# Attention by pairs of heads on the two halves of the array

## The chip, the cores and the metric

One core of a Trainium2 chip runs the whole program in one launch. The metric is the device time of a run in microseconds (us), the median of three runs. The engines have short names in the profile: PE (TensorE, matrix products), PEld (its weight loads), DVE (VectorE), ACT (ScalarE), POOL (GpSimd) and SP (which issues the DMAs). One matrix product needs its stationary operand loaded into the 128 x 128 array and streams the moving operand through it. A product whose operands cover 64 rows, or whose result covers 64 columns, takes half the array.

## The reference

Two blocks of two layers each work on 512 tokens of width 1024. Attention is 8 heads of width 64 in both.

```python
# block 1, per layer: window of 128 with a sink; head h reads key/value group h // 4
s = einsum(q_block, k_band) * 64 ** -0.5          # query block of 128 against 2 x 128 keys
p = softmax(concat([where(mask, s, -inf), sink]))[..., :-1]
ya = (p @ v_band) @ w_a
r = chunkwise_retention(rq, rk, rv)               # 4 heads
x = x + (sigmoid(ga) * ya + sigmoid(gb) * (norm(r) * silu(rg)) @ w_b) @ w_out
x = x + square(relu(norm(x) @ w_up)) @ w_down
# block 2, per layer: an indexer selects keys, then attention, then gated linear attention
score = einsum(relu(q_idx . k_idx), w_idx)        # 8 index heads of width 64
p = softmax(where(in_top_128(score), q k / 8, -inf)); ya = (p @ v) @ p_attn
state = decay * state + k_dec^T v; o = q state    # chunks of 64 tokens, 4 heads
```

## The kernel before, in words

Activations lie feature-major: eight tiles of 128 features by 512 tokens. Products with the big weights run in three passes (`k_step`, lines 387 to 394): operands are split into a high and a low part, and high x high, low x high and high x low are added in PSUM. A main unit is one output tile: 8 input tiles x 3 passes = 24 products of 512 columns (`fm`, line 404); in `tm` (line 435) it is a token tile against 256 weight columns, 24 products of 256 columns, with a burst behind every second one.

All small work is run beside these units by `Pump` (lines 214 to 252), which has six lanes. A job is a generator that alternates between a step that issues products and a step that issues what reads them. After each main unit `unit_done` (line 370) calls `products()`, which takes one products step of every lane in lane order, so that these products stand in TensorE's queue as one burst behind the unit; then it emits the unit's own evacuation, then `results()`, and then `top_up`, the split of the next weight piece into high and low (ACT line 328, DVE line 329). Everything is in program order on its engine; a wait in a burst holds the next main unit too.

An attention job has three products steps: the scores (`mm3`, lines 396 to 402, three passes of 64 rows), the transposes of the probabilities (line 541), and the products with V (lines 612 and 1088, results of 64 columns; each is two instructions, since these operands are plain float32). Between scores and transposes lies the softmax: mask and maximum on DVE (578 and 1069), exponential on ACT (589 and 1075), reciprocal and scaling on DVE (546 and 548).

- `attn1` (line 561, block 1): one job takes one query block of 128 tokens and two heads of the same key group; both heads' scores use the same 64 rows. 16 jobs per layer in lanes 0 to 2. The two heads' products with V go to different halves of the columns (`64 * j`, line 613).
- `attn2` (line 1057, block 2): one job takes one query block b with 128 * (b + 1) keys. For b < 2 it holds two heads (h0 and h0 + 2, which lie in the same half), for b >= 2 one. 24 jobs per layer in lanes 0 to 2.
- `index` (line 1023): per pair of heads three passes of the even head (rows 0 to 63), then three of the odd one (rows 64 to 127), in two PSUM banks.
- `gla` (line 1155): per 128 tokens two chunks c of 64 tokens, each on its half of the rows: 6 products of c = 0, then 6 of c = 1, twice; then 8 products with the states (line 1195), c outermost.

PSUM has 2 banks for main units and 6 for the side work (`side_ps`).

Of the kernel before, what the change touches and what calls it, by code (L numbers as in the profile page):

```python
# [19 lines left out]
P = 128  # L20
# [9 lines left out]
PAD = 24  # L30
# [42 lines left out]
def _weights_1(a, l):  # L73
    w = a["w_in"][l]
    aq = w[:, 0:512].reshape(D, 8, 64)[:, :, _ROPE]
    aq = np.stack([aq[:, 0:4], aq[:, 4:8]], axis=2).reshape(D, 512)
    ak = w[:, 512:640].reshape(D, 2, 64)[:, :, _ROPE].reshape(D, 128)
    s = []
    s += _fm(aq) + _fm(ak) + _fm(w[:, 640:768])
    s += _fm(w[:, 768:1280]) + _fm(w[:, 1280:1792])  # L80
    s += _tm(w[:, 1792:2816])
    s += _fm(w[:, 3840:4864])
    s += _fm(a["w_a"][l])
# [79 lines left out]
def layout(a):  # L163
# [11 lines left out]
    for l in range(DEPTH):  # L175
        sm.add(f"g_mix{l}", _cols(a["g_mix"][l]))
        sm.add(f"g_mlp{l}", _cols(a["g_mlp"][l]))
        sm.add(f"sink{l}", np.broadcast_to(a["sinks"][l][None, :], (P, 8)))
# [76 lines left out]
class Net:  # L255
# [287 lines left out]
    def normalize(self, sp, parts, sm):  # L543

        rc = self.tiny(len(parts))
        self.nc.vector.reciprocal(rc, sm)
        for i, s in enumerate(parts):
            self.nc.vector.tensor_scalar(sp[:, s], sp[:, s], rc[:, i : i + 1], None, op0=ALU.mult)

    def head_done(self, st, f, n):  # L550

        st["pv"][f][1] += n
        if st["pv"][f][1] == 8:
# [7 lines left out]
    def attn1(self, b, f, aq, st, l):  # L561

        nc = self.nc
        g, i = f // 2, f % 2
        nk = 1 if b == 0 else 2
        w = nk * P
        r = slice(64 * g, 64 * g + 64)
        at = [slice(j * 256, j * 256 + w) for j in range(2)]
        ps = self.side_ps()
        for j in range(2):  # L570
            self.mm3(
                ps[:, at[j]], aq[2 * i + j], st["ak"], r,
                slice(b * P, (b + 1) * P), slice((b + 1 - nk) * P, (b + 1) * P),
            )
        yield
        sp, mr, sm = self.s(), self.tiny(2), self.tiny(2)
        for j in range(2):
            nc.vector.tensor_tensor_reduce(
                out=sp[:, at[j]], in0=ps[:, at[j]],
                in1=self.band[:, 256 - w : 256], scale=1.0, scalar=-3.0e38,  # L580
                op0=ALU.add, op1=ALU.max, accum_out=mr[:, j : j + 1],
            )
        sink = self.small(f"sink{l}")[:, 2 * f : 2 * f + 2]
        m, nm, d = self.tiny(2), self.tiny(2), self.tiny(2)
        nc.vector.scalar_tensor_tensor(m, mr, 0.125, sink, op0=ALU.mult, op1=ALU.max)
        nc.vector.tensor_scalar(nm, m, -1.0, None, op0=ALU.mult)
        nc.vector.tensor_tensor(d, sink, m, op=ALU.subtract)
        for j in range(2):
            nc.scalar.activation(
                sp[:, at[j]], sp[:, at[j]], AF.Exp,  # L590
                bias=nm[:, j : j + 1], scale=0.125, accum_out=sm[:, j : j + 1],
            )
        nc.scalar.activation(d, d, AF.Exp)
        nc.vector.tensor_tensor(sm, sm, d, op=ALU.add)
        self.normalize(sp, at, sm)
        yield
        pt = self.side_ps()
        for s in at:
            self.transposes(pt[:, s], [sp[:, s.start + k * P : s.start + (k + 1) * P] for k in range(nk)])
        yield  # L600
        PT = self.s()
        if nk == 2:
            nc.scalar.copy(PT, pt)
        else:
            for s in at:
                nc.scalar.copy(PT[:, s], pt[:, s])
        yield
        pv = self.head_bank(st, f)
        for j in range(2):
            for k in range(nk):  # L610
                o = (b + 1 - nk + k) * P + 64 * g
                nc.tensor.matmul(
                    pv[64 * j : 64 * j + 64, b * P : (b + 1) * P], lhsT=st["V"][:, o : o + 64],
                    rhs=PT[:, at[j].start + k * P : at[j].start + (k + 1) * P], start=(k == 0), stop=(k == nk - 1),
                )
        yield
        self.head_done(st, f, 2)
        yield

# [92 lines left out]
    def layer_1(self, l, x, nx):  # L712
# [30 lines left out]
        def ev_kv(o, ps):  # L743
# [7 lines left out]
            else:  # L751
                av = self.s()
                nc.vector.tensor_tensor(av, ps, st["R"], op=ALU.mult)
                self.pump.add(0, self.vtrans(av, st, "V"))
                n = 0
                for f0 in (0, 2):
                    for b in range(4):
                        for f in (f0, f0 + 1):
                            if 0 < n < 3:
                                self.pump.add(n, self.idle(3-n))  # L760
                            self.pump.add(n % 3, self.attn1(b, f, aq, st, l))
                            n += 1
# [260 lines left out]
    def index(self, b, iq, st):  # L1023
# [33 lines left out]
    def attn2(self, b, hs, aq, ak, st):  # L1057

        nc = self.nc
        n = (b + 1) * P  # L1060
        r = slice(64 * (hs[0] % 2), 64 * (hs[0] % 2) + 64)
        at = [slice(i * n, (i + 1) * n) for i in range(len(hs))]
        ps = self.side_ps()
        for s, h in zip(at, hs):
            self.mm3(ps[:, s], aq[h // 2], ak[h // 2], r, slice(b * P, (b + 1) * P), slice(0, n))
        yield
        sp, mr, sm, nm = self.s(), self.tiny(len(hs)), self.tiny(len(hs)), self.tiny(len(hs))
        for i, s in enumerate(at):
            nc.vector.tensor_tensor_reduce(
                out=sp[:, s], in0=ps[:, s], in1=st["bias"][b], scale=1.0, scalar=-3.0e38,  # L1070
                op0=ALU.add, op1=ALU.max, accum_out=mr[:, i : i + 1],
            )
        nc.vector.tensor_scalar(nm, mr, -0.125, None, op0=ALU.mult)
        for i, s in enumerate(at):
            nc.scalar.activation(sp[:, s], sp[:, s], AF.Exp, bias=nm[:, i : i + 1], scale=0.125, accum_out=sm[:, i : i + 1])
        self.normalize(sp, at, sm)
        yield
        pt = self.side_ps()
        w = n * len(hs)
        self.transposes(pt, [sp[:, k * P : (k + 1) * P] for k in range(w // P)])  # L1080
        yield
        PT = self.s()
        nc.scalar.copy(PT[:, :w], pt[:, :w])
        yield
        for s, h in zip(at, hs):
            pv = self.head_bank(st, h // 2)
            for k in range(b + 1):
                nc.tensor.matmul(  # L1088
                    pv[64 * (h % 2) : 64 * (h % 2) + 64, b * P : (b + 1) * P], lhsT=st["V"][k][:, h * 64 : (h + 1) * 64],
                    rhs=PT[:, s.start + k * P : s.start + (k + 1) * P], start=(k == 0), stop=(k == b),  # L1090
                )
        yield
        for h in hs:
            self.head_done(st, h // 2, 1)
        yield

    def gla_gates(self, glr, wg, gk, st):
# [4 lines left out]
        for t0 in (0, 2):  # L1102
            pp = [self.side_ps(), self.side_ps()]
            for i in range(2):
                t = t0 + i
                self.mm3(pp[i], glr, wg, slice(0, 33), slice(t * P, (t + 1) * P), FULL)
# [48 lines left out]
    def gla(self, gq, kd, gv, st):  # L1155
# [8 lines left out]
        for t in range(4):  # L1164
            kds, gvs = nxt
            pk = [[self.side_ps(), self.side_ps()] for _ in range(2)]
            for i in range(2):
                for c in range(2):
                    r = slice(64 * c, 64 * c + 64)
                    for j in range(2):  # L1170
# [20 lines left out]
            for i in range(2):  # L1191
                for c in range(2):
                    for j in range(2):
# [29 lines left out]
    def layer_2(self, l, xs, iq, wgd, last):  # L1223
# [83 lines left out]
        for h0 in (0, 4):  # L1307
            even, odd = (h0, h0 + 2), (h0 + 1, h0 + 3)
            for b in range(4):
                for hs in (even, odd) if b < 2 else ((h0,), (h0 + 1,), (h0 + 2,), (h0 + 3,)):  # L1310
                    if n < 3:
                        self.pump.add(n, self.wait([3], n))
                    self.pump.add(n % 3, self.attn2(b, hs, aq, ak, st))
                    n += 1
# [269 lines left out]
def emit(nc, meta, arrays, stop=None):  # L1584
# [4 lines left out]
    with tile.TileContext(nc) as tc:  # L1589
        with (  # L1590
# [8 lines left out]
            stack.enter_context(tc.tile_pool(name="pad", bufs=1)).tile([P, PAD], F, name="pad")  # L1599
# [53 lines left out]
```

## Time and profile before

| | us |
|---|---|
| median of 3 runs (3393.69 to 3393.78) | 3393.76 |
| the profiled execution's own time | 3394.25 |
| its span | 3392.5 |
| PE busy | 3348.3 (99%) |
| PEld busy | 2818.3 (83%) |
| DVE busy | 1965.2 (58%) |
| ACT busy | 1292.1 (38%) |
| POOL busy | 657.0 (19%) |

The span is the time between the first and the last instruction of the profiled execution; its own time is 1.75 us longer. The ends of matmuls are modelled and overlap the next, so that PE's busy share tells that it hardly stands still, not that each product is at its fastest. In the timeline the first column is the start of an instruction; what a product costs is the distance to the next start. The granted clock is 0.996 of full speed on the mean.

### The profile page before, as it was taken

What the parts mean: (1) busy time and instruction counts of PE and PEld (TensorE: products, weight loads), DVE (VectorE), ACT (ScalarE), POOL (GpSimd) and SP (SyncE); (2) the same over time, 40 slices, a digit from 0 to 9 for tenths busy, and PEclk for the clock granted to TensorE, in tenths of its full rate; (3) what the DMA queues carried; (4) which work ended last, traced back from release to release, by engine and by line L of the source; (5) the groups of instructions that cost most, each with busy time, mean ns of one, the idle gap of its engine ahead of it and who ended that gap; (6) DMA issues with size and microseconds to landing.
All of it is one profiled execution on the core that took longest, in us unless ns stands there. A gap on an engine that the chain in (4) does not pass through costs nothing.

```text
span 3392.5 us, 43066 instructions
## 1 busy us (share of the span) xinstructions
PE 3348.3 (99%) x17450; PEld 2818.3 (83%) x17450; DVE 1965.2 (58%) x3435; ACT 1292.1 (38%) x2206; POOL 657.0 (19%) x447
## 2 busy tenths in 40 slices
PE   9999999999999999999999999999999999999998
PEld 7888888887888888889988778888889777888887
DVE  7555543457555553456884447555778744575466
ACT  3433333233333343333533344343354333443342
POOL 5100000123100010031550013210146400232113
PEclk9999999999999999999999999999999999999998
DMA  4222222232122222231212131223212122312230
GB/s 150 75 75 78 97 100 100 99 125 75 51 75 75 100 103 97 91 136 52 81 70 75 63 124 50 87 100 126 98 52 75 63 75 75 124 41 97 100 137 26
DMA packets 44935, 295.93 MB, mean 87 GB/s; under 512 B 5120, under 2 KB 7296, under 8 KB 10816
## 3 DMA queue, kind: packets, MB, share of 16 engines
q1 hardware_dynamic: 44496, 292.66, 24.1%
q8 instruction: 137, 2.24, 0.3%
q14 instruction: 62, 0.51, 0.0%
q0 software_dynamic: 80, 0.26, 0.0%
q10 hardware_dynamic: 160, 0.26, 0.0%
HBM read 291.06 MB, written 2.10 MB: 86 GB/s over the span
## 4 chain that ended last, share of the span: by engine, by line
PE 92%; DVE 5%; issue 1%; ACT 1%; POOL 0%; DMA 0%; DVEq 0%; SPq 0%; ACTq 0%; POOLq 0%
PE pm L392 22%; PE pm L393 22%; PE pm L394 22%; PE ps L392 3%; PE ps L394 3%; PE ps L393 3%; PE pm L445 3%; PE pm L446 3%; PE pm L447 3%; PE ps L541 2%; PE ps L400 1%; PE ps L1088 1%; DVE s L1008 1%; PE ps L401 1%; PE ps L402 1%
## 5 line engine op out<-in xcount | busy, mean ns | idle before, releaser
L392 PE MATMUL pm<-xh,hi 128*128 128x512 f32 (+1 forms) x3056 | 1193.4, 391 | 3.8 <-DVE c L1407 3.0
L393 PE MATMUL pm<-xl,hi 128*128 128x512 f32 (+1 forms) x3056 | 1181.4, 387 | 1.6 <-DVE xl L1560 1.1
L394 PE MATMUL pm<-xh,lo 128*128 128x512 f32 (+1 forms) x3056 | 1180.7, 386 | 0.4 <-DVE lo L329 0.4
L392 PEld LDWEIGHTS pm<-xh,hi 128*128 128x128 f32 x3056 | 573.9, 188 | 127.3 <-issue 12.3
L394 PEld LDWEIGHTS pm<-xh,lo 128*128 128x128 f32 x3056 | 573.9, 188 | 118.5 <-DVE lo L329 0.8
L393 PEld LDWEIGHTS pm<-xl,hi 128*128 128x128 f32 x3056 | 574.3, 188 | 115.5 <-DVE xl L1560 3.2
L329 DVE TENSOR_TENSOR lo<-raw,hi 128x1024 fp32r<-128x1024 f32 (+1 forms) x413 | 516.8, 1254 | 173.0 <-ACT hi L328 172.2
L328 ACT CAST hi<-raw 128x1024 fp32r<-128x1024 f32 (+1 forms) x469 | 483.0, 1035 | 205.7 <-PE pm L393 165.3
L445 PE MATMUL pm<-hi,xh 128*128 128x256 f32 x768 | 221.0, 288 | 0.8 <-DVE s L1006 0.7
L446 PE MATMUL pm<-lo,xh 128*128 128x256 f32 x768 | 217.3, 283 | 0.0
L447 PE MATMUL pm<-hi,xl 128*128 128x256 f32 x768 | 217.1, 283 | 0.0
L392 PE MATMUL pm<-xh,whi 128*128 128x512 f32 (+1 forms) x512 | 186.6, 365 | 4.1 <-DVE s L534 4.1
L393 PE MATMUL pm<-xl,whi 128*128 128x512 f32 (+1 forms) x512 | 186.2, 364 | 0.8 <-DVE xl L1560 0.5
L394 PE MATMUL pm<-xh,wlo 128*128 128x512 f32 (+1 forms) x512 | 185.4, 362 | 0.0
L1415 POOL TENSOR_TENSOR c<-c,c 128x512 f32<-128x512 f32 x44 | 84.3, 1916 | 500.7 <-DVE c L1407 477.6
L329 POOL TENSOR_TENSOR lo<-raw,hi 128x1024 fp32r<-128x1024 f32 x56 | 140.8, 2515 | 128.8 <-ACT hi L328 108.7
L445 PEld LDWEIGHTS pm<-hi,xh 128*128 128x128 f32 x768 | 147.1, 192 | 8.0 <-issue 2.7
L446 PEld LDWEIGHTS pm<-lo,xh 128*128 128x128 f32 x768 | 147.3, 192 | 0.2
L447 PEld LDWEIGHTS pm<-hi,xl 128*128 128x128 f32 x768 | 147.2, 192 | 0.0
L392 PE MATMUL ps<-xh,hi 128*128 128x512 f32 (+1 forms) x384 | 138.7, 361 | 7.3 <-ACT hi L328 7.3
L498 POOL TENSOR_TENSOR s<-s,s 128x512 f32<-128x512 f32 x26 | 34.9, 1343 | 567.7 <-ACT s L495 567.5
L1406 DVE SCALAR_TENSOR_TENSOR c<-pm,smalls,c 128x511 f32<-128x511 f32 x82 | 61.4, 749 | 135.0 <-ACT c L1405 134.8
(318 smaller groups left out, 4779.3 us busy)
## 6 DMA issues: line engine op xcount, KB each, us to landing
raw<-w SPq DMA_DIRECT2D x265, 1024.0 KB, 4.8
raw<-w SPq DMA_DIRECT2D x7, 768.0 KB, 4.4
x<-x SPq DMA_DIRECT2D x8, 256.0 KB, 7.0
out<-acc SPq DMA_DIRECT2D x16, 128.0 KB, 1.8
raw<-w SPq DMA_DIRECT2D x2, 896.0 KB, 4.5
s<-big SPq DMA_DIRECT2D x6, 256.0 KB, 5.6
raw<-w SPq DMA_DIRECT2D x2, 512.0 KB, 5.1
smalls<-small SPq DMA_DIRECT2D x1, 462.5 KB, 7.5
```

Of the source, the lines that this page charges most:

```text
L328: self.nc.scalar.copy(hi[:, :n], raw)
L329: e.tensor_tensor(lo[:, :n], raw, hi[:, :n].bitcast(F), op=ALU.subtract)
L392: mm(ps[:, ts], lhsT=w1, rhs=xh[:, ts], start=first, stop=False)
L393: mm(ps[:, ts], lhsT=w1, rhs=xl[:, ts], start=False, stop=False)
L394: mm(ps[:, ts], lhsT=w2, rhs=xh[:, ts], start=False, stop=last)
L445: self.nc.tensor.matmul(ps[:, :256], lhsT=x1, rhs=w1, start=(k == 0), stop=False)
L446: self.nc.tensor.matmul(ps[:, :256], lhsT=x1, rhs=w2, start=False, stop=False)
L447: self.nc.tensor.matmul(ps[:, :256], lhsT=x2, rhs=w1, start=False, stop=(k == NK - 1))
L498: (e or self.nc.gpsimd).tensor_tensor(acc, acc, sq, op=ALU.add)
L541: self.nc.tensor.transpose(dst[:, i * P : (i + 1) * P], src, self.ident)
L1406: nc.vector.scalar_tensor_tensor(c[:, 1:], ps[:, : T - 1], w[1], c[:, 1:], op0=ALU.mult, op1=ALU.add)
L1415: nc.gpsimd.tensor_tensor(a, a, c, op=ALU.mult)
```

## The change

One function `attend` takes the place of `attn1`'s and `attn2`'s bodies. A job now takes one pair f of heads, one on each half of the rows (g = 0 and 1), and one or two query blocks. Scores of the two heads go to two banks, pass by pass in turn; the probabilities are transposed into two banks; the products with V take turns between the two column halves. In block 1 a pair is a head of key group 0 and the same head of key group 1 (the rows of `w_a` are put in that order on the host), and a job takes blocks (0, 1) or (2, 3): 8 jobs per layer in lanes 0 and 1. In block 2 a job takes blocks (0, 1), (2) or (3): 12 jobs per layer in lanes 0 and 1. The width of the unused tile `pad` is computed so that what follows the table of small constants keeps its address.

```diff
-    def mm3(self, ps, a, b, rows, ca, cb):
-        (ah, al), (bh, bl) = a, b
-        mm(ps, lhsT=ah[rows, ca], rhs=bh[rows, cb], start=True, stop=False)
-        mm(ps, lhsT=ah[rows, ca], rhs=bl[rows, cb], start=False, stop=False)
-        mm(ps, lhsT=al[rows, ca], rhs=bh[rows, cb], start=False, stop=True)
+    def mm3(self, *jobs):
+        for i, j in ((0, 0), (0, 1), (1, 0)):
+            for ps, a, b, rows, ca, cb in jobs:
+                mm(ps, lhsT=a[i][rows, ca], rhs=b[j][rows, cb], start=(i == j), stop=(i == 1))
...
-        if st["pv"][f][1] == 8:
+        if st["pv"][f][1] == 4:
...
+    def attend(self, f, blocks, q, k, v, st, sink=None):
+        nc = self.nc
+        segs, o = [], 0
+        for b, k0, nk, mask in blocks:
+            segs.append((b, k0, nk, mask, slice(o, o + nk * P)))
+            o += nk * P
+        rows = [slice(0, 64), slice(64, P)]
+        ps = [self.side_ps(), self.side_ps()]
+        for b, k0, nk, mask, at in segs:
+            self.mm3(*[
+                (ps[g][:, at], q, k, rows[g], slice(b * P, (b + 1) * P), slice(k0 * P, (k0 + nk) * P))
+                for g in range(2)
+            ])
+        yield
+        n = 2 * len(segs)
+        sp, mr, sm, nm = [self.s(), self.s()], self.tiny(n), self.tiny(n), self.tiny(n)
+        parts = [(g, sg[3], sg[4]) for g in range(2) for sg in segs]
+        for i, (g, mask, at) in enumerate(parts):
+            nc.vector.tensor_tensor_reduce(
+                out=sp[g][:, at], in0=ps[g][:, at], in1=mask, scale=1.0, scalar=-3.0e38,
+                op0=ALU.add, op1=ALU.max, accum_out=mr[:, i : i + 1],
             )
...
+        for i, (g, mask, at) in enumerate(parts):
+            nc.scalar.activation(
+                sp[g][:, at], sp[g][:, at], AF.Exp,
+                bias=nm[:, i : i + 1], scale=0.125, accum_out=sm[:, i : i + 1],
             )
+        if sink is not None:
+            nc.scalar.activation(d, d, AF.Exp)
+            nc.vector.tensor_tensor(sm, sm, d, op=ALU.add)
+        rc = self.tiny(n)
+        nc.vector.reciprocal(rc, sm)
+        for i, (g, mask, at) in enumerate(parts):
+            nc.vector.tensor_scalar(sp[g][:, at], sp[g][:, at], rc[:, i : i + 1], None, op0=ALU.mult)
+        yield
+        pt = [self.side_ps(), self.side_ps()]
+        for g in range(2):
+            self.transposes(pt[g], [sp[g][:, j * P : (j + 1) * P] for j in range(o // P)])
+        yield
+        PT = [self.s(), self.s()]
+        for g in range(2):
+            nc.scalar.copy(PT[g][:, :o], pt[g][:, :o])
         yield
         pv = self.head_bank(st, f)
+        for b, k0, nk, mask, at in segs:
+            for j in range(nk):
+                for g in range(2):
+                    nc.tensor.matmul(
+                        pv[rows[g], b * P : (b + 1) * P], lhsT=v(k0 + j, g),
+                        rhs=PT[g][:, at.start + j * P : at.start + (j + 1) * P], start=(j == 0), stop=(j == nk - 1),
+                    )
+        yield
+        self.head_done(st, f, len(segs))
+        yield
...
+                self.pump.add(1, self.idle(2))
                 n = 0
+                for f in range(4):
+                    for bs in ((0, 1), (2, 3)):
+                        self.pump.add(n % 2, self.attn1(f, [band(b) for b in bs], aq, st, l))
+                        n += 1
...
-            for h, ps in zip((h0, h0 + 1), pss):
-                r = slice(64 * (h % 2), 64 * (h % 2) + 64)
-                self.mm3(ps[:, :n], iq[h // 2], st["ik"], r, slice(b * P, (b + 1) * P), slice(0, n))
+            self.mm3(*[
+                (ps[:, :n], iq[h0 // 2], st["ik"], slice(64 * g, 64 * g + 64), slice(b * P, (b + 1) * P), slice(0, n))
+                for g, ps in enumerate(pss)
+            ])
...
             for i in range(2):
-                for c in range(2):
-                    r = slice(64 * c, 64 * c + 64)
-                    for j in range(2):
-                        h = 2 * i + j
-                        js = slice(j * 256, (j + 1) * 256)
-                        self.mm3(pk[i][c][:, js], kds, gvs[i], r, slice(h * P, (h + 1) * P), js)
+                for j in range(2):
+                    h = 2 * i + j
+                    js = slice(j * 256, (j + 1) * 256)
+                    self.mm3(*[
+                        (pk[i][c][:, js], kds, gvs[i], slice(64 * c, 64 * c + 64), slice(h * P, (h + 1) * P), js)
+                        for c in range(2)
+                    ])
...
-                for c in range(2):
-                    for j in range(2):
+                for j in range(2):
+                    for c in range(2):
                         js = slice(j * 256, (j + 1) * 256)
...
+        for f in range(4):
+            for bs in ((0, 1), (2,), (3,)):
+                if n < 2:
+                    self.pump.add(n, self.wait([3], n))
+                self.pump.add(n % 2, self.attn2(f, bs, aq, ak, st))
+                n += 1
```

## Rows read from the trace of the kernel before

**Rows 1.** The page: busy time, share of the span and instructions of each engine.
```profile
PE 3348.3 (99%) x17450; PEld 2818.3 (83%) x17450; DVE 1965.2 (58%) x3435; ACT 1292.1 (38%) x2206; POOL 657.0 (19%) x447
```
**Rows 2.** PE's longest wait: engine, line, releaser; us in total, times, longest.
```profile
PE ps L1195 <- DVE S L1185: 7.6, 2, 3.8
```
**Rows 3.** Timeline of PE, block 2's first scores: start, us, engine, line, form.
```profile
1812.08 0.39 PE L393 MATMUL pm<-xl,hi 128*128 128x512 f32 x1
1812.30 0.39 PE L394 MATMUL pm<-xh,lo 128*128 128x512 f32 x1
...
1813.12 0.27 PE L401 MATMUL ps<-xl,xh 64*128 64x128 f32 x1
1813.23 0.27 PE L402 MATMUL ps<-xh,xl 64*128 64x128 f32 x1
...
1813.77 0.39 PE L393 MATMUL pm<-xl,hi 128*128 128x512 f32 x1
```
**Rows 4.** Timeline of PE, a burst of index scores.
```profile
1615.64 0.39 PE L394 MATMUL pm<-xh,lo 128*128 128x512 f32 x1
...
1616.53 0.40 PE L402 MATMUL ps<-xh,xl 64*128 64x512 f32 x2
1616.76 0.35 PE L400 MATMUL ps<-xh,xh 64*128 64x384 f32 x2
1616.94 0.34 PE L401 MATMUL ps<-xl,xh 64*128 64x384 f32 x2
...
1617.42 0.28 PE L401 MATMUL ps<-xl,xh 64*128 64x256 f32 x2
1617.54 0.28 PE L402 MATMUL ps<-xh,xl 64*128 64x256 f32 x2
...
1618.09 0.40 PE L393 MATMUL pm<-xl,hi 128*128 128x512 f32 x1
```
**Rows 5.** Timeline of PE, block 1's products with V alone in a burst.
```profile
186.42 0.39 PE L394 MATMUL pm<-xh,lo 128*128 128x512 f32 x1
186.74 0.67 PE L612 MATMUL ps<-s,V 128*64 128x128 f32 x8
...
187.68 0.40 PE L393 MATMUL pm<-xl,hi 128*128 128x512 f32 x1
```
**Rows 6.** Timeline of PE, a burst of block 2's attention with all kinds of work.
```profile
1888.53 0.39 PE L394 MATMUL pm<-xh,lo 128*128 128x512 f32 x1
...
1890.18 1.09 PE L1088 MATMUL ps<-s,V 128*64 128x128 f32 x8
1891.92 0.39 PE L393 MATMUL pm<-xl,hi 128*128 128x512 f32 x1
```
**Rows 7.** Timeline of PE, linear attention's 24 products of one burst.
```profile
1737.64 0.39 PE L394 MATMUL pm<-xh,lo 128*128 128x512 f32 x1
...
1739.36 0.28 PE L402 MATMUL ps<-xh,xl 64*128 64x256 f32 x2
...
1740.26 0.39 PE L393 MATMUL pm<-xl,hi 128*128 128x512 f32 x1
```
**Rows 8.** Timeline of DVE, softmax of a block 1 job (two heads).
```profile
82.37 0.41 DVE L578 CUSTOM_DVE_ANT_0 s<-ps,s 128x256 f32<-128x256 f32 x1
...
86.28 0.61 DVE L548 TENSOR_SCALAR s<-s,t 128x256 f32<-128x256 f32 x2
```
**Rows 9.** Timeline of PE, that job's transposes, first of their burst.
```profile
88.78 0.49 PE L541 MATMUL ps<-smalls,s 128*128 128x128 f32 x3
```
**Rows 10.** Timeline of ACT, that job's first exponential.
```profile
84.67 0.51 ACT L589 ACTIVATE s<-s,t 128x256 f32<-128x256 f32 x1 [8.40 <-DVE t L586]
```
**Rows 11.** Timeline of DVE, softmax of a block 2 job (one head, 512 keys).
```profile
1899.88 0.69 DVE L1069 CUSTOM_DVE_ANT_0 s<-ps,score 128x512 f32<-128x512 f32 x1 [0.18 <-PE ps L402]
...
1901.90 0.49 DVE L548 TENSOR_SCALAR s<-s,t 128x512 f32<-128x512 f32 x1
```
**Rows 12.** Timeline of PE, the first product of the burst behind it.
```profile
1905.85 0.32 PE L400 MATMUL ps<-xh,xh 64*128 64x128 f32 x1
```

More of the change, by code (lines that the diff above doesn't have):

```diff
@@ L29 @@
 AHEAD_1, AHEAD_2 = 9, 11
-PAD = 24
 TOP_ROUNDS = 2
@@ L177, in layout @@
         sm.add(f"g_mlp{l}", _cols(a["g_mlp"][l]))
-        sm.add(f"sink{l}", np.broadcast_to(a["sinks"][l][None, :], (P, 8)))
+        pairs = np.repeat(a["sinks"][l].reshape(2, 4).T, 2, axis=1).reshape(1, 16)
+        sm.add(f"sink{l}", np.broadcast_to(pairs, (P, 16)))
     sm.add("g_final", _cols(a["g_final"]))
@@ L559, in head_bank @@
         return st["pv"][f][0]
-    def attn1(self, b, f, aq, st, l):
+    def attend(self, f, blocks, q, k, v, st, sink=None):
         nc = self.nc
[L564 to L569, printed above, removed]
-        for j in range(2):
-            self.mm3(
-                ps[:, at[j]], aq[2 * i + j], st["ak"], r,
-                slice(b * P, (b + 1) * P), slice((b + 1 - nk) * P, (b + 1) * P),
-            )
-        yield
-        sp, mr, sm = self.s(), self.tiny(2), self.tiny(2)
-        for j in range(2):
[L578 to L595, printed above, removed]
-        yield
[L597 to L606, printed above, removed]
@@ new lines, in attend @@
+        sp, mr, sm, nm = [self.s(), self.s()], self.tiny(n), self.tiny(n), self.tiny(n)
[4 more added lines that the diff above has]
+                op0=ALU.add, op1=ALU.max, accum_out=mr[:, i : i + 1],
+            )
+        if sink is None:
+            nc.vector.tensor_scalar(nm, mr, -0.125, None, op0=ALU.mult)
+        else:
+            m, d = self.tiny(n), self.tiny(n)
+            nc.vector.scalar_tensor_tensor(m, mr, 0.125, sink, op0=ALU.mult, op1=ALU.max)
+            nc.vector.tensor_scalar(nm, m, -1.0, None, op0=ALU.mult)
+            nc.vector.tensor_tensor(d, sink, m, op=ALU.subtract)
@@ L607, in attn1 @@
+        yield
+        pt = [self.side_ps(), self.side_ps()]
+        for g in range(2):
+            self.transposes(pt[g], [sp[g][:, j * P : (j + 1) * P] for j in range(o // P)])
+        yield
+        PT = [self.s(), self.s()]
+        for g in range(2):
+            nc.scalar.copy(PT[g][:, :o], pt[g][:, :o])
         yield
         pv = self.head_bank(st, f)
[L609 to L615, printed above, removed]
+        for b, k0, nk, mask, at in segs:
[4 more added lines that the diff above has]
+                        rhs=PT[g][:, at.start + j * P : at.start + (j + 1) * P], start=(j == 0), stop=(j == nk - 1),
+                    )
@@ L616, in attn1 @@
         yield
-        self.head_done(st, f, 2)
+        self.head_done(st, f, len(segs))
         yield
+    def attn1(self, f, blocks, aq, st, l):
+        v = lambda k, g: st["V"][:, k * P + 64 * g : k * P + 64 * g + 64]
+        yield from self.attend(f, blocks, aq[f], st["ak"], v, st, self.small(f"sink{l}")[:, 4 * f : 4 * f + 4])
     def vtrans(self, src, st, key):
@@ L754, in ev_kv @@
                 self.pump.add(0, self.vtrans(av, st, "V"))
+                band = lambda b: (b, max(0, b - 1), min(b + 1, 2), self.band[:, 128 if b == 0 else 0 : 256])
+                self.pump.add(1, self.idle(2))
                 n = 0
[L756 to L762, printed above, removed]
+                for f in range(4):
+                    for bs in ((0, 1), (2, 3)):
+                        self.pump.add(n % 2, self.attn1(f, [band(b) for b in bs], aq, st, l))
+                        n += 1
         self.fm(xs, 2, ev_kv)
@@ L1055, in index, with attn2 @@
             yield
[L1057 to L1095, printed above, removed]
+    def attn2(self, f, bs, aq, ak, st):
+        v = lambda k, g: st["V"][k][:, f * P + 64 * g : f * P + 64 * g + 64]
+        yield from self.attend(f, [(b, 0, b + 1, st["bias"][b]) for b in bs], aq[f], ak[f], v, st)
     def gla_gates(self, glr, wg, gk, st):
@@ L1191, in gla @@
             for i in range(2):
-                for c in range(2):
-                    for j in range(2):
+                for j in range(2):
+                    for c in range(2):
                         js = slice(j * 256, (j + 1) * 256)
@@ L1306, in layer_2 @@
         n = 0
[L1307 to L1314, printed above, removed]
+        for f in range(4):
[4 more added lines that the diff above has]
+                n += 1
         sil, tga, tgb = [None] * 8, [None] * 8, [None] * 8
@@ L1598, in emit @@
             smalls = const.tile([P, arrays["small"].shape[1]], F, name="smalls")
-            stack.enter_context(tc.tile_pool(name="pad", bufs=1)).tile([P, PAD], F, name="pad")
+            pad = (24 - (arrays["small"].shape[1] - 928)) % P or P
+            stack.enter_context(tc.tile_pool(name="pad", bufs=1)).tile([P, pad], F, name="pad")
             hi = stack.enter_context(tc.tile_pool(name="hi", bufs=HI_BUFS))
```

10 lines of the change are left out of this document (2 added, 8 removed).

## The prediction

> **What bounds the kernel now.** I read the page's busy shares first: PE is busy 99% of the span, DVE 58%, ACT 38% [rows 1]. Then the waits of PE: the longest group is 7.6 us, in linear attention, and the change leaves what it waits for as it is [rows 2]. So TensorE's queue sets the time, and a product that takes fewer nanoseconds there shortens the run, as long as what the product reads is ready. What is left is to see what a product costs, and for that the timeline is read by the distance from one start to the next. Main products follow each other at 0.22 to 0.23 us (1812.08 to 1812.30 [rows 3]; I take 0.227, a unit of 24 being 5.45 us). From the last product of a unit to the second one of the next there would be two such steps, 0.454 us, without a burst; what is more is the burst's cost.
>
> Four prices come out. (a) Scores of one head: 128 columns follow at 0.11 us (1813.12 to 1813.23) [rows 3]. (b) Scores in the index: the rows say x2. Products of the two halves start together and the pair takes one step: 0.23 us for 512 columns (1616.53 to 1616.76), 0.18 for 384, 0.12 for 256 [rows 4]. There, program order is three products of one half, then three of the other. The two halves run side by side all the same. (c) Products with V: eight instructions take 0.67 us in block 1, whose two heads write different column halves [rows 5], and 1.09 us in block 2, whose heads write one half or come alone [rows 6]. (d) Each change between full-array and half-array work, or between row halves and column halves, costs extra. A burst of six scores alone costs 1813.77 - 1812.30 - 0.454 = 1.01 us, of which 6 x 0.11 = 0.66 are steps: 0.35 for two changes, 0.175 each [rows 3]. The burst of [rows 6] has 8 transposes (0.11 a step, as three last 0.49 with one of 0.27 [rows 9]), 3 scores of 512 and 8 instructions with V at 0.11: 3.39 - 0.454 less 0.88, 0.69 and 0.88 is 0.49, or 0.16 for each of three changes. Transposes use the full array and change nothing beside a main product. I take 0.175.
>
> **The change part by part.** All counts are from the loops, the two layers of each block taken together.
>
> *Scores of block 1.* Per layer 24 products of 128 columns and 72 of 256, one after another: 24 x 0.11 + 72 x 0.12 = 11.3 us. In pairs half of that goes; two layers save 11.3 us.
>
> *Scores of block 2.* Per head 3 x (0.11 + 0.12 + 0.18 + 0.23) = 1.92 us, eight heads 15.4; half goes in each of two layers: 15.4 us. No row shows a pair of 128 columns. Its step lies between 0.11 (as a 256-column pair keeps the single's step) and 0.22 (no overlap); the second would take back 24 pairs x 0.11 x 2 blocks = 5.3 us. I take 0.11, the nearest row being the 256-column pair.
>
> *Products with V.* Block 1 is paired already, so nothing changes. Block 2 has 16 heads (two layers) x 10 products x 2 instructions = 320, that is 40 times eight; each eight goes from 1.09 to 0.67: 40 x 0.42 = 16.8 us.
>
> *Bursts and changes of the array.* Before, a layer of block 1 has 18 bursts (59.69 to 186.74 us in the first layer) and block 2 has 26 (1812.62 to 2006.99), with three lanes in different steps. Written out by kind and counted, they have 53 and 82 changes. After, two lanes hold 4 and 6 jobs of three steps each, the second lane one unit later: 13 and 19 bursts. They run in cycles of (transposes, scores), (V, transposes), (scores, V), with 2 + 2 + 3 changes, or 29 and 43 in all. That saves 2 x (53 + 82 - 29 - 43) = 126 changes x 0.175 = 22.0 us. The transposes keep their number.
>
> *What pairs cost.* An index burst costs 1618.09 - 1615.64 - 0.454 = 2.00 us with 3 x 0.53 = 1.59 in steps, so 0.41 for its two changes against 0.35 for single scores [rows 3, 4]. I charge the 0.06 to each of the 40 new jobs (8 x 2 and 12 x 2): 2.4 us.
>
> *Index scores.* They are x2 before the edit, so taking turns in program order gains nothing [rows 4]: 0, with 0.1 us either way for each of ten bursts. The Trainium skill speaks otherwise: "TensorE: Matmul & The Clock Gate", section "The mechanism" of Part 3, says matmuls start and end in strict program order and only weight loads are pulled ahead of them. By that rule only one product of three would overlap before the edit; the trace disagrees, as the second half's first product starts with the first half's first one.
>
> *Linear attention.* Six products of one half stand ahead of six of the other, and the rows turn to x2 only after the third. A burst costs 1740.26 - 1737.64 - 0.454 = 2.17 us [rows 7]. With all 24 in pairs it is 12 x 0.12 + 0.41 = 1.85. Eight such bursts save 2.6 us. The products with the states (line 1195) wait for DVE's states, whose order stays [rows 2]: 0, between a loss of 0.4 and a gain of 0.6 us for each of eight bursts.
>
> *Softmax.* A job's softmax now has two heads and up to four parts between two bursts, and TensorE stands if the transposes come first. In block 1 two parts of 256 run from 82.37 to 86.89 [rows 8], ahead of the transposes at 88.78 [rows 9]. Two more add 2 x 0.35 (mask and maximum, 0.41 long with overlap), 2 x 0.5 (exponential [rows 10]) and 2 x 0.31 (scaling [rows 8]) = 2.3: 89.2. The new bursts are shorter, so that the transposes would be called at about 88.6 and the second bank's 0.4 later. Such a job is late by some 0.2 us. This holds for the 5 jobs per layer beside units whose evacuation is rope on DVE, 10 in all: 2 us. Bounds: 0, if DVE has no other delay, and 15, if a weight split (some 1.2 us on DVE) falls into the chain each time. In block 2 the softmax of 512 keys ends at 1902.39, 3.5 us ahead of the next burst [rows 11, 12]; a second head adds 0.6 + 0.7 + 0.5 = 1.8, and the shorter burst takes about 1: still early, 0.
>
> Splits, evacuations and DMAs move with their units and are hidden under PE; the softmax has fewer small operations, which DVE has room for [rows 1].
>
> **Sum.** 11.3 + 15.4 + 16.8 + 22.0 - 2.4 + 2.6 - 2.0 = 63.7 us off the profiled execution's 3394.25: 3330.6. The median lies 0.5 lower, so 3330 us.
>
> **Rivals.**
>
> *Softmax late in block 1.* DVE's evacuation, weight split and the four-part chain fill a whole unit, so each of the 10 jobs holds TensorE by 1.5 us instead of 0.2: 3330 + 13 = 3343. For it: two parts already end only 1.9 us ahead [rows 8, 9]. Against: every third unit has no softmax and catches up. "TensorEngine Tiling (Array Packing)", section "PSUM Bottleneck", of the Trainium skill warns of the same: tiling speeds the products, not what reads their banks.
>
> *The pairs don't run together in the attention jobs,* so the change doesn't do what it says. Then scores, V and linear attention save nothing, only the 22.0 of array changes less 2.0 remain: 3374. For it: no row shows attention scores in pairs. Against: index and block 1's V do it [rows 4, 5].
>
> *Slower.* In both blocks the transposes wait for the softmax of two heads in all 40 jobs. It decides from 65.7 / 40 = 1.6 us a job (the gain without the 2 us charged above); at 2.5 us it takes 100, and the time is 3394 - 66 + 100 = 3428. For it: one chain through DVE, ACT and DVE, twice as wide. Against: block 2 has 3.5 us in hand [rows 11, 12].
>
> *Array changes cheaper still.* If a pair's first step hides its change, the 2.4 and part of the 29 + 43 changes go too (2 x 72 x 0.05 = 7): 3321.
>
> *Products start in program order after all,* and the starts in the rows x2 are not when the halves really work. Then an index burst of six products of one width cost five steps and will cost three; a layer's index has 8 x 3 x (0.12 + 0.18 + 0.23) = 12.7 us of single steps, a third of it goes in each of two layers, 8.5 us: 3322. That is the skill's rule cited at the index. Against: 2.00 us for 18 products, which single steps of 3.2 us don't allow, nor five sixths of them, 2.65 [rows 4].
>
> **Chances.** Forecast 70%, softmax late 15%, pairs apart 4%, slower 4%, cheaper changes 5%, program order 2%. The forecast's own range is 3324 to 3338; the stated one reaches to the cheaper changes and the late softmax, 3320 to 3350, and takes in the unseen pair (5.3) and the states (-3 to +5); with some 15% outside. About 0.2% (7 us) is what a measurement tells from no change; all but the slower case lie clear of it, with 1% left between.
>
> **What would show it.** After, attention scores in the timeline say x2; eight V instructions of block 2 take 0.67 us; bursts number 13 and 19 a layer; index bursts cost 2.0 as before; linear attention's 24 products cost 1.85. A wait of PE on line 541's transposes for DVE's scaling, above 0.2 us a job, shows the late softmax. Single scores in the new jobs, or PE's idle time above 40 us, would make it wrong.

## The result, and the profile after

The changed kernel takes 3336.05 us (median of four runs, 3334.57 to 3336.14), the kernel before 3393.73 beside it. The ratio is 0.983 [0.9813, 0.9847]: a gain of 57.7 us. The prediction said 63.7 us less and 3330; the time is 6 us above that. The profiled execution is the fastest of the four, 3334.57 us, at a mean granted clock of 0.996; against the profiled execution of before, 3394.25, that is 59.7 us.

TensorE is still the engine that sets the time; its busy share is 98% where it was 99% [rows 1]:

```profile
PE 3280.2 (98%) x17450; PEld 2771.7 (83%) x17450; DVE 1931.4 (58%) x3307; ACT 1285.0 (39%) x2182; POOL 657.1 (20%) x447
```

The same 17450 instructions take 68.1 us less of TensorE's time. DVE and ACT have fewer instructions, as the softmax's small operations now serve twice as many parts (a head in one query block) at a time.

Now the four kinds of small products, in the timeline of TensorE after (start, us, engine, line, form). First the index, linear attention, block 2's first scores and its last products with V:

```profile
1599.70 0.39 PE L394 MATMUL pm<-xh,lo 128*128 128x512 f32 x1
1600.02 0.50 PE L402 MATMUL ps<-xh,xh 64*128 64x512 f32 x2
...
1602.14 0.40 PE L393 MATMUL pm<-xl,hi 128*128 128x512 f32 x1
...
1721.69 0.39 PE L394 MATMUL pm<-xh,lo 128*128 128x512 f32 x1
1722.01 0.38 PE L402 MATMUL ps<-xh,xh 64*128 64x256 f32 x2
...
1723.96 0.40 PE L393 MATMUL pm<-xl,hi 128*128 128x512 f32 x1
...
1795.88 0.39 PE L394 MATMUL pm<-xh,lo 128*128 128x512 f32 x1
1796.19 0.33 PE L402 MATMUL ps<-xh,xh 64*128 64x128 f32 x2
1796.36 0.28 PE L402 MATMUL ps<-xl,xh 64*128 64x128 f32 x2
1796.47 0.28 PE L402 MATMUL ps<-xh,xl 64*128 64x128 f32 x2
...
1797.42 0.39 PE L393 MATMUL pm<-xl,hi 128*128 128x512 f32 x1
...
1930.88 1.09 PE L610 MATMUL ps<-s,V 128*64 128x128 f32 x16
```

Read each as in the prediction: the distance from the main product ahead to the second one behind, less 0.454. The index costs 1602.14 - 1599.70 - 0.454 = 1.99, as before [rows 4]. Linear attention's 24 products cost 1.82 where they took 2.17 [rows 7]. Block 2's first job now says x2, and its pairs of 128 columns follow each other at 0.11 us (1796.36 to 1796.47): the pair that no row of before showed costs what a single product costs [rows 3]. With V, sixteen instructions take the 1.09 us that eight took [rows 6].

Added up over all bursts in that way, from the two timelines (where the main products have 256 columns, their step is about 0.11 in place of 0.227, and less is taken off): block 1's two layers go from 65.6 to 47.7 us (13 bursts a layer), block 2's from 110.6 to 65.3 (19 a layer; the transposes for other work that share these bursts are left out on both sides), linear attention's eight from 17.4 to 14.6. That is 66.0 us; the prediction's terms for the bursts, with what it took off for the late softmax, make 63.7. So TensorE's own work became at least as much cheaper as was said, and some was lost again. The waits of TensorE in the profile after show where (engine, line, releaser; us in total, times, longest):

```profile
PE ps L1164 <- DVE S L1154: 8.2, 4, 3.8
PE ps L392 <- ACT hi L328: 8.0, 1, 8.0
PE pm L392 <- DVE s L534: 4.8, 2, 4.1
...
PE pm L392 <- ACT hi L328: 3.0, 2, 1.5
...
PE pm L392 <- ACT xh L458: 1.8, 2, 1.2
```

The first row is the wait of [rows 2], in four pieces for two; the second and third stood there before, within 0.7 us. The last two are new. Neither is in the attention: they are main products of other units that wait for ACT. Two smaller rows on line 445, left out here, are new or longer and are taken up below.

**The wait in block 1.** ACT and then TensorE in the profile after, behind the first layer's retention (the figure in brackets is idle time ahead, with its releaser):

```profile
230.46 0.84 ACT L685 ACTIVATE rv<-ps,t 128x256 f32<-128x256 f32 x2 [2.23 <-DVE t L483]
231.19 2.94 ACT L328 CAST hi<-raw 128x1024 fp32r<-128x1024 f32 x3
```

```profile
232.36 0.39 PE L394 MATMUL pm<-xh,lo 128*128 128x512 f32 x1
234.23 0.47 PE L392 MATMUL pm<-xh,hi 128*128 128x512 f32 x1 [1.49 <-ACT hi L328]
```

ACT first waits 2.23 us for DVE to give the factors for the two scalings of retention's last step, and three weight splits stand behind it in its queue. TensorE wants the last one at 232.6 and gets it at 234.13 (231.19 + 2.94). In the kernel before, the units that project the attention's output met the results of retention's third step of four (its line 682, at 241.19). By then ACT had made its splits ahead: one split stood behind the results, and for the next ACT waited 0.59 us until TensorE freed a buffer:

```profile
241.19 0.84 ACT L682 ACTIVATE rv<-ps,t 128x256 f32<-128x256 f32 x2 [2.39 <-DVE t L483]
241.92 1.05 ACT L328 CAST hi<-raw 128x1024 fp32r<-128x1024 f32 x1
243.56 1.04 ACT L328 CAST hi<-raw 128x1024 fp32r<-128x1024 f32 x1 [0.59 <-PE pm L393]
```

Attention takes fewer units now and retention is released by its end, so that each of retention's steps falls three units (72 main products) earlier. Now the last step's results fall on those output units, with their splits still to be made. From 232.36 to 234.23 are 1.87 us, of which 0.227 are the usual step: 1.65 us, in each layer, 3.3 in all.

**The wait in block 2.** ACT, DVE and TensorE in the profile after, where linear attention's last gated output (sil, the input of main units to come) meets the softmax of a job with four parts:

```profile
1895.96 0.40 ACT L586 ACTIVATE s<-s,t 128x128 f32<-128x128 f32 x1 [1.62 <-DVE t L579]
...
1899.77 0.63 ACT L458 ACTIVATE xh<-sil 128x512 fp32r<-128x512 f32 x1 [1.95 <-DVE sil L1188]
```

```profile
1898.07 1.01 DVE L596 TENSOR_SCALAR s<-s,t 128x128 f32<-128x128 f32 x4
1898.99 0.75 DVE L1188 SCALAR_TENSOR_TENSOR sil<-ps,smalls,sil 128x512 f32<-128x512 f32 x1
```

```profile
1892.57 1.03 PE L541 MATMUL ps<-smalls,s 128*128 128x128 f32 x8
...
1899.50 0.39 PE L394 MATMUL pm<-xh,lo 128*128 128x512 f32 x1
1900.45 0.50 PE L392 MATMUL pm<-xh,hi 128*128 128x512 f32 x1 [0.57 <-ACT xh L458]
1901.18 0.50 PE L393 MATMUL pm<-xl,hi 128*128 128x512 f32 x1 [0.23 <-DVE xl L459]
```

DVE takes its work in the order of the program: it waits for the exponentials of all four parts, scales them, and only at 1898.99 makes sil. ACT then splits sil into xh, DVE makes xl, and the last products of the running main unit read both. In the kernel before this split began 4.9 us behind the start of its burst (1914.11 to 1918.98), here 7.2 (1892.57 to 1899.77). The rows of before, of PE and ACT:

```profile
1914.11 0.38 PE L541 MATMUL ps<-smalls,s 128*128 128x128 f32 x2
```

```profile
1918.98 0.63 ACT L458 ACTIVATE xh<-sil 128x512 fp32r<-128x512 f32 x1 [1.53 <-DVE sil L1219]
```

TensorE loses 1.2 us in this layer (1901.18 - 1899.50 less two steps) and 1.9 in the other, 3.1 in all. Together the two places take 6.4 us, and 66.0 - 6.4 = 59.6 is close to the 59.7 us between the two profiled executions. That the two agree to 0.1 us is partly chance. TensorE's other rows of waits are 2.7 us longer in sum than before: for one, main products on line 445 now wait 0.5 us for ACT's copy of V (line 1271), which stands behind linear attention's scaling (line 1179), and their wait for DVE on line 1008 goes from 0.7 to 1.4 us. What made up for these was not traced.

### The profile page after: what moved, and what is told of

It reads as the page before. It is cut to its first block, busy times and chain, and to the rows that moved or that the text cites. A ratio compares the mean times of both kernels' runs of the same rounds, so it can differ in the third digit from the quotient of the medians.

```text
span 3332.8 us, 42963 instructions
## 1 busy us (share of the span) xinstructions
PE 3280.2 (98%) x17450; PEld 2771.7 (83%) x17450; DVE 1931.4 (58%) x3307; ACT 1285.0 (39%) x2182; POOL 657.1 (20%) x447
## 3 DMA queue, kind: packets, MB, share of 16 engines
q8 instruction: 137, 2.24, 0.3%
## 4 chain that ended last, share of the span: by engine, by line
PE 92%; DVE 5%; ACT 1%; issue 1%; POOL 0%; DMA 0%; SPq 0%; DVEq 0%; ACTq 0%; POOLq 0%
PE pm L392 22%; PE pm L393 22%; PE pm L394 22%; PE ps L392 3%; PE ps L394 3%; PE ps L393 3%; PE pm L445 3%; PE pm L446 3%; PE pm L447 3%; PE ps L402 2%; PE ps L541 2%; PE ps L610 1%; DVE s L1010 1%; PE ps L1164 0%; PE ps L661 0%
## 5 line engine op out<-in xcount | busy, mean ns | idle before, releaser
L339 DVE TENSOR_TENSOR wlo<-raw,whi 128x512 fp32r<-128x512 f32 x162 | 128.8, 838 | 18.0 <-ACT whi L338 17.4
```

The source lines that it names most:

```text
L339: e.tensor_tensor(los[q][:, :m], r, his[q][:, :m].bitcast(F), op=ALU.subtract)
```

## Experiments

Each kernel was timed in five rounds beside the kernel before (3393.57, 3393.50 and 3393.74 us in the three sets). The first set asks whether the two new waits are the missing 6 us, against the rival that attention itself pays for them.

**e0_after**, the changed kernel again. 

> The changed kernel once more, as the base for the three others on the same chip: 3336.0 us by every theory (3334.6 to 3336.1 so far).

Measured: 3335.51 us (3334.77 to 3336.12), ratio 0.9828 [0.9815, 0.9842]. The base of the comparisons below.

**e1_ret_later**: block 1's retention starts three units after attention's end, about where it stood before.

```diff
-        self.pump.add(4, self.wait([0, 1, 2]))
+        self.pump.add(4, self.wait([0, 1, 2], 3))
```

> Retention starts three units later, as far from the attention's end as the kernel before had it. Theory (the missing 6 us are two new waits outside the attention): its last step's results no longer stand ahead of the weight splits of the short attention-output units, the wait of 1.65 us on ACT's split goes in both layers of block 1, 3.3 us: 3332.7. Rival (the missing 6 us are bursts that cost more than their steps, or a slower stream everywhere): no change, 3336.0, with retention's bursts only moved.

Measured: 3333.40 us (3331.62 to 3333.66), ratio 0.9822 [0.9809, 0.9836]: 2.1 less than e0, ranges apart. The row of 3.0 us on line 328 is gone from TensorE's waits and the one on line 458 stays. The sign and the row are as expected, the size is two thirds of it; the runs of e0 and e1 spread over 1.4 and 2.0 us, so the 1.2 us that lack are not clear of noise.

**e2_attn2_later**: block 2's attention one unit later against the main units, retention as in the changed kernel.

```diff
-                    self.pump.add(n, self.wait([3], n))
+                    self.pump.add(n, self.wait([3], n + 1))
```

> Block 2's attention starts one unit later, so that the last unit ahead of linear attention's output projection has a softmax of two parts of 512 keys instead of four parts. Theory: the last gated row's split on ACT comes in time, the waits of 1.2 and 1.9 us go, 3.1 us in all: 3332.9. Rival (as for the run before): 3336.0. Against the theory in part would be 3334.5, if the two-part softmax is late too.

Measured: 3331.89 us (3331.45 to 3332.75), ratio 0.9818 [0.9805, 0.9831]: 3.6 less, 3.1 expected. Now the row on line 458 is gone and that of 3.0 on line 328 is there. Attention that only starts a unit later, with the same work, is worth this much.

**e3_both_later**: both edits. 

> Both delays together. Theory: both savings add, 6.4 us: 3329.6, what the prediction's sum gives. Rival: 3336.0.

Measured: 3329.53 us (3329.28 to 3330.64), ratio 0.9811 [0.9798, 0.9825]: 6.0 less than e0. Its waits of TensorE have neither row:

```profile
PE ps L1164 <- DVE S L1154: 8.2, 4, 3.8
PE ps L392 <- ACT hi L328: 7.7, 1, 7.7
PE pm L392 <- DVE s L534: 4.9, 2, 4.1
...
PE pm L445 <- ACT V L1271: 1.4, 2, 0.8
```

and on its ACT, the output units meet the results of retention's third step again, as in the kernel before, with one split at a time behind them:

```profile
231.14 0.84 ACT L685 ACTIVATE rv<-ps,t 128x256 f32<-128x256 f32 x2 [2.40 <-DVE t L483]
231.87 1.05 ACT L328 CAST hi<-raw 128x1024 fp32r<-128x1024 f32 x1
233.51 1.05 ACT L328 CAST hi<-raw 128x1024 fp32r<-128x1024 f32 x1 [0.58 <-PE pm L393]
```

So the two waits are the missing 6 us: with both away, the kernel stands where the prediction put it. That it stands there to 0.5 us is partly chance, as the bursts saved 2.3 us more than their terms said and other waits took some of it: the waits of TensorE sum to 35.6 us here and to 32.8 before the change. No version here is faster beyond the noise.

The second set takes the change's own parts, one at a time.

**e4_no_turns**: the three products of one half, then those of the other, with each segment's halves still next to each other. The attention by pairs stays.

```diff
-        for i, j in ((0, 0), (0, 1), (1, 0)):
-            for ps, a, b, rows, ca, cb in jobs:
+        for ps, a, b, rows, ca, cb in jobs:
+            for i, j in ((0, 0), (0, 1), (1, 0)):
```

> Only the taking of turns within the scores is undone: each job still holds a pair, but the three products of one half stand ahead of the three of the other, segment by segment (attention, index, linear attention). Theory (the halves run side by side as long as the other half's products stand within some three products): no change against the changed kernel on this chip, within 0.5 us, and pairs still start together in the trace. Rival (products start in program order, so that the turns make the gain): one third of the pairs' gain in scores is lost, some 9 us in attention and 8 us in the index, 3353.

Measured: 3334.96 us (3334.69 to 3335.53), ratio 0.9827 [0.9813, 0.9841]: no change. Its timeline of TensorE in the index, with three products of one half ahead of the other's in program order:

```profile
1600.49 0.50 PE L402 MATMUL ps<-xh,xh 64*128 64x512 f32 x2
...
1601.29 0.35 PE L402 MATMUL ps<-xh,xh 64*128 64x384 f32 x2
```

Both halves still start together. The time bears out what the rows x2 say: with starts in program order it would have been some 3353 us, by the rival's sum. Here the Trainium skill's "TensorE: Matmul & The Clock Gate", Part 3, "The mechanism", expects strict program order of the matmuls; these rows and the time differ from it.

**e5_half_by_half**: scores of all segments of one head, then of the other; products with V likewise. Up to six products of scores, or eight instructions with V, of one half now stand ahead of the other's.

```diff
-        for b, k0, nk, mask, at in segs:
-            self.mm3(*[ ... for g in range(2)])
+        for g in range(2):
+            for b, k0, nk, mask, at in segs:
+                self.mm3((ps[g][:, at], q, k, rows[g], ...))
...
-        for b, k0, nk, mask, at in segs:
-            for j in range(nk):
-                for g in range(2):
+        for g in range(2):
+            for b, k0, nk, mask, at in segs:
+                for j in range(nk):
```

> In the attention jobs all products of one half are issued ahead of all of the other, scores and products with V (up to 8 ahead). Theory (the other half is reached only some three products ahead, as linear attention showed before): scores of 6 ahead lose three steps, 0.33 us, 24 times; products with V lose two to five steps of 0.11: in all some 20 us, 3356 (3346 to 3362). Rival (the halves run freely, whatever the order): 3336.

Measured: 3355.62 us (3354.99 to 3356.05), ratio 0.9888 [0.9874, 0.9902]: 20 us more than e0. Its timeline of TensorE, block 2's first scores and last products with V:

```profile
1807.93 0.32 PE L402 MATMUL ps<-xh,xh 64*128 64x128 f32 x1
1808.09 0.27 PE L402 MATMUL ps<-xl,xh 64*128 64x128 f32 x1
1808.21 0.27 PE L402 MATMUL ps<-xh,xl 64*128 64x128 f32 x1
1808.21 0.44 PE L402 MATMUL ps<-xh,xh 64*128 64x128 f32 x2
...
1946.94 1.58 PE L608 MATMUL ps<-s,V 128*64 128x128 f32 x16
```

The second head's first product, seventh in the program, starts 0.28 us behind the first head's first, beside its third. It passes three that have not begun. Two run alone at the front, and as many at the end; that burst cost 1.37 us, against 1.09 in the changed kernel. Sixteen instructions with V take 1.58 us for 1.09. So the halves do run apart from program order, but in these rows only over some three products (three ahead cost nothing in e4, six ahead cost 0.28 us here); beyond that the order of the program decides. Taking turns is one way to keep them near.

**e6_gla_undone**: linear attention's two loops back in the old order (half outermost).

```diff
-                for j in range(2):
-                    h = 2 * i + j
...
-                    self.mm3(*[ ... for c in range(2)])
+                for c in range(2):
+                    for j in range(2):
+                        h = 2 * i + j
...
+                        self.mm3((pk[i][c][:, js], kds, gvs[i], ...))
...
-                for j in range(2):
-                    for c in range(2):
+                for c in range(2):
+                    for j in range(2):
```

> Only linear attention's order is put back to half by half. Theory: its eight bursts of 24 products cost 2.16 instead of 1.82 us (+2.7), its products with the states lose what turns cost them in the first two steps (3.04 back to 2.70 and 8.27 back to 8.06, -1.1 in two layers): +1.7, 3337.7. Rival (turns cost the states nothing, the difference was the later start of DVE's states): +2.7, 3338.7.

Measured: 3337.59 us (3337.06 to 3338.23), ratio 0.9835 [0.9821, 0.9849]: 2.1 more than e0; eight bursts are back at 2.16 us each for 1.82, which is 2.7. The first states' burst of a layer goes from 3.04 back to 2.69. That looked as if turns made the products with the states dearer, and was put to e8.

**e7_single_blocks**: block 2's short jobs by single query blocks, so that pairs stay but bursts go from 38 to 50.

```diff
-            for bs in ((0, 1), (2,), (3,)):
+            for bs in ((0,), (1,), (2,), (3,)):
```

> Block 2's attention takes one query block per job, 16 jobs instead of 12 a layer: the same products in 25 bursts instead of 19, with 57 array changes instead of 43. Theory: 28 changes of 0.175 in two layers and 8 more pairs at 0.06 add 5.4 us to the bursts; the softmax ahead of the output projection has two parts of 256 instead of four parts, ends 1.6 us earlier and the 3.1 us of waits go: +2.3, 3338.3. Rival (changes cost less than 0.1 us, and the missing time is in them): +2 in the bursts, 3335 or 3338 with or without the waits.

Measured: 3336.75 us (3336.12 to 3337.67), ratio 0.9832 [0.9818, 0.9846]: 1.2 more than e0, 2.3 expected. The bursts sum to 69.9 us for 65.3: 4.6 us, which by the expectation's 28 changes and 8 pairs at 0.06 is 0.15 for each change in place of 0.175 (0.16, if a pair costs nothing more). The wait on line 458 is gone, as the jobs fall on other units, and gives 3.1 back: 4.6 - 3.1 = 1.5. Without the rows of the waits one would read from the time that more bursts cost almost nothing.

The third set has e3 as its base, and asks what is still left.

**e10_both_again**, the kernel of e3. 

> The kernel with both delays again, as the base for the two others on the same chip: 3329.5 us by every theory.

Measured: 3329.88 us (3328.62 to 3330.09), ratio 0.9811 [0.9797, 0.9824].

**e8_states_back**: e3 with the products with the states alone in the old order.

```diff
-                for j in range(2):
-                    for c in range(2):
+                for c in range(2):
+                    for j in range(2):
```

> Both delays, and linear attention's products with the states in the old order (chunk by chunk), its scores in turns as changed. Theory (these products wait for DVE's states, which come chunk by chunk, so turns only put a product that is not ready ahead of one that is): the first states' burst goes from 3.04 back to 2.70 us in both layers, 0.7 to 1.1 us in all: 3328.7. Rival (the later start of the states costs it, whatever the order): 3329.5.

Measured: 3330.04 us (3329.18 to 3330.64), ratio 0.9811 [0.9798, 0.9825]: no change. The first states' burst in e8, then in the kernel after and in the kernel before (timelines of TensorE):

```profile
1727.35 2.90 PE L1164 MATMUL ps<-S,gq 128*64 128x256 f32 x16
```

```profile
1729.29 0.65 PE L1164 MATMUL ps<-S,gq 128*64 128x256 f32 x2
1730.25 1.94 PE L1164 MATMUL ps<-S,gq 128*64 128x256 f32 x14 [0.32 <-DVE S L1154]
```

```profile
1745.59 2.57 PE L1195 MATMUL ps<-S,gq 128*64 128x256 f32 x16
```

The order is the old one and the burst is as long as with turns (2.90 us, for 1729.29 to 1732.19 in the kernel after). That theory fell. What remains is that the states come when DVE has made them: TensorE, 0.34 us earlier thanks to the scores' burst, waits that much longer for them. The first step's gain is given back on the spot. The traces bear this out: DVE's first state begins 8.04 to 8.06 us behind the last main product ahead of the scores' burst, whether that burst is long (before, 1737.64 to 1745.70; e6) or short (after, 1721.69 to 1729.73; e8). No run moved the states by themselves.

**e9_attn1_later**: e8 with block 1's attention two units later.

```diff
-                self.pump.add(1, self.idle(2))
+                self.pump.add(0, self.idle(2))
+                self.pump.add(1, self.idle(4))
```

> As the run before, and block 1's attention starts two units later, so that three instead of five of its softmaxes a layer lie beside units whose evacuation is rope on DVE. Theory (bursts of block 1 that cost 0.2 to 0.5 us more than their steps wait for the scaling of single parts): 0.5 to 1.2 us less than the run before, 3327.9. Rival (those bursts are long for another reason): no change, 3328.7.

Measured: 3329.42 us (3328.88 to 3329.66), ratio 0.9810 [0.9796, 0.9823]: 0.6 under e8 with ranges that overlap. The long bursts of the first jobs came along (2.24 and 2.01 us in the new place, 2.22 and 1.99 in the old); one later burst went from 2.00 to 1.83. The sums differ by 0.15 us. A miss: the first jobs' delay doesn't hang on which main units stand beside them. For the very first job of a layer the rows of the kernel after say what it does hang on; compare its burst (scores from 58.68, transposes from 65.36) with the third job's, whose evacuation beside it is the same:

```profile
80.41 0.33 PE L402 MATMUL ps<-xh,xh 64*128 64x128 f32 x2
...
81.29 1.09 PE L610 MATMUL ps<-s,V 128*64 128x128 f32 x16
87.90 0.82 PE L541 MATMUL ps<-smalls,s 128*128 128x128 f32 x6
```

DVE begins the scaling 6.24 us behind the start of the scores in both (64.92 and 86.65). But TensorE comes to the transposes after 6.5 us in the first job (64.92 + 0.227, less 58.68) and after 7.5 in the third, as no products with V stand behind the first job's scores. In e9 these scores still stand alone, which fits that nothing changed. This is read from rows; no run tried it, and the smaller delays of later jobs stay open.

## Why the prediction was right, and where it failed

**Bound.** Right: TensorE is busy 98% and its price per product decides. The forecast's likeliest case held, 6 us off, inside its own range of 3324 to 3338.

**Scores, V, changes of the array, pairs.** Right in mechanism and, within 3 us, in sum; no run tells these terms apart. Block 1's bursts were to save 11.3 + 8.4 (48 of the changes) - 1.0 - 2.0 = 16.7 us and saved 17.9; block 2's 15.4 + 16.8 + 13.7 (78 changes) - 1.4 = 44.4, and saved 45.3. V was priced by durations, 1.09 to 0.67; by steps of 0.11, as the other terms are, it would have been 17.6 for the 16.8. The unseen pair of 128 columns came out at the end that was taken, 0.11. The number of bursts, 13 and 19, is exact. The price of a change was read from two rows as 0.175 and 0.16; e7 gives 0.15 to 0.16. Of such changes the Trainium skill ("TensorEngine Tiling (Array Packing)", "Key Properties") says that changing the tiling mode drains the engine; that a change costs time agrees with it and this is its price here, but no run shows that the cost is a drain.

**Index.** Right: 1.99 us, nothing gained, and e4 shows for the whole kernel that the order within three products of a half is worth nothing (3334.96 for 3335.51 us). Of the two parts of the change, "by pairs of heads" is the gain; "taking turns" matters only where more than some three products of a half would otherwise stand ahead, as e5 shows with 20 us and linear attention with its 2.1 to 2.7.

**Linear attention.** 1.82 a burst for the 1.85 predicted. The states, put at 0 within -0.4 and +0.6, lost 0.34 in the first burst of each layer, as DVE's first state comes no earlier (e8).

**Softmax late.** Right in kind and mostly in size: some 1.3 us for 2.0, in four bursts instead of ten. The profile after shows it in the transposes of the first jobs, in TensorE's and DVE's timelines:

```profile
64.92 0.39 PE L394 MATMUL pm<-xh,lo 128*128 128x512 f32 x1
65.36 1.06 PE L541 MATMUL ps<-smalls,s 128*128 128x128 f32 x6
66.35 0.39 PE L402 MATMUL ps<-xh,xh 64*128 64x256 f32 x2
```

```profile
64.92 1.01 DVE L596 TENSOR_SCALAR s<-s,t 128x128 f32<-128x128 f32 x4
```

The scaling runs from 64.92 to 65.93 and the transposes begin at 65.36, part by part behind it; six take 1.06 us where five steps of 0.11 and one of 0.27 make 0.82. This burst costs 2.22 us, the same one without delay 1.76. That no row of the waits names it shows why such a delay is looked for in the steps of the timeline. The rival by which it would hold up all ten jobs by 1.5 us is out.

**The step that failed.** "Splits, evacuations and DMAs move with their units and are hidden under PE." They do move with their units, but what else moves is not asked there: attention gets through in fewer units, so retention, released by its end, comes earlier against the main units, and the wider softmax holds DVE's queue for longer. ACT and DVE work here in the order of the program, and in both places a short operation that the next main unit needs stood behind a chain of the side work that was waiting for the other engine. Busy shares of 58% and 38% [rows 1] were taken as room; they say nothing of that. e1 to e3 moved the side work by some units and nothing else, and 6.0 of the 6.0 us came back. In the single runs e1 gave 2.1 of its 3.3 us and e2 3.6 of 3.1; differences of 1.2 and 0.5 us are within the spread of one kernel's runs (up to 2.0 us), so they settle nothing.

**Left open.** The lesser delays of later jobs' transposes, the waits on line 445 (1.4 us for ACT's V in e3), and how much of the bursts' gain belongs to each term.

## What to carry to other kernels

Price small products by the step from start to start and by the changes around their burst, and pair heads on the two halves wherever one head at a time uses half the array: with rows of both kinds, the sum came out to 4% here (63.7 for 66.0). Once such work takes fewer units, list everything that is released by its end or shares a queue with it, and check its place against the main units; a delay of one to three units was worth 6 us here, a tenth of the whole gain. When an experiment changes the number of units, read its waits before its time, as a stall that comes or goes can hide its price (e7).

## What the runs showed of the hardware

In these traces the two halves of the array start products out of program order with respect to each other, over some three products: side by side with three ahead (e4, index), 0.28 us behind with six ahead (e5, scores). A pair of half-array products of 128 columns takes the 0.11 us of a single one. And sixteen instructions with V on both column halves run in eight steps, 1.09 us, but take 1.58 when the program orders them by half.
